# Key and value weights loaded ahead of the rope rows, a spread moved behind another row's products, two rows normalised in halves, and new rank offsets in a planned single-core decoder block

## The chip, the core and the metric

The kernel runs on one core of a Trainium2 chip. The time is the device time of one execution in microseconds; the median of several executions is what counts. PE is the matrix engine (TensorE), PEld its weight loads, DVE the vector engine, ACT the scalar engine, POOL the general-purpose vector engine (GpSimd), and SP the queue that issues nearly all transfers. Each of them works through its own list in the written order.

## The reference

One decoder block on x of 1024 rows by 1024 columns, all in float32:

```
h = RMSNorm(x)
qa, ka, va, q_lat, kv_lat, k_r, g_a, g_b = split(h @ w_in)      # 512|128|128|384|256|32|1024|1024
A = sliding-window attention(rope(qa), rope(ka), va, sinks)       # window 128, 8 heads on 2 key heads
q = RMSNorm(q_lat) @ w_uq        # 8 heads x (64 plain + 32 rope), rope on the 32
k, v = RMSNorm(kv_lat) @ w_ukv   # 8 heads x (64 key + 64 value); one 32-wide rope key for all heads
B = causal attention([q, rope q], [k, rope k_r], v)
x = x + (sigmoid(g_a) * (A @ w_o_swa) + sigmoid(g_b) * (B @ w_o_mla)) @ w_out
x = x + (silu(RMSNorm(x) @ w_gate) * (RMSNorm(x) @ w_up)) @ w_down
out = RMSNorm(x)
```

## The kernel before

Every large product is done in three passes (`mm3`, lines 311 to 313 of the profile). An operand is split into a high part, which ACT writes as a rounded copy (`CAST`), and a low part, the difference, which DVE (sometimes POOL) writes; PE then multiplies high by high, high by low and low by high into one PSUM bank. Larger matrix products also use a seven-product scheme, whose sums and differences of blocks are DVE and POOL work. The 1024 rows of x are eight blocks of 128, called rows 0 to 7 here.

The order of work is written down by a planner, the class `Plan`. A step has a name such as `("nm", 1)`, an engine (E for PE, A for ACT, D for DVE, P for POOL, S for SP, J for a bookkeeping step that emits nothing), a cost, the steps that it comes after, a rank, and the buffers that it takes and gives back. `run` keeps a clock for each engine, and always emits the step that could start first; among those that could start within a slack of each other it takes the one with the lowest rank. Costs, ranks and the constants `TAIL` and `HOP` (what an engine's end and a hand-over are reckoned at) therefore only set the order of instructions in each engine's list. There are three plans, one behind the other:

- `beg`, the first 305 us of the span: the normalisation of x, the latent query rows, the projections, the gates and the sliding-window attention. Here the ranks come from the time by which a step is needed, and the table `SHIFT` adds an offset for each kind of step.
- `pre`, the next 33 us or so: transposes of the latent rows (`lT`), the rope part of the queries (`r`, then `ra`, `rj`, `rq`), splits of the query weights (`a`) and of the key and value weights (`b`), the last gates, and the first query product. Its ranks are a position plus the offset in `PRANK`.
- `plan`, up to about 530 us: the latent attention with its scores (`scb`), softmax (`p`), transposes (`pTb`), output products (`ob`), and the products that make queries, keys and values, with the table `RANK`.

The rest of the span (output projections and the feed-forward part) is not touched.

In the start of `beg` a row b is treated thus. ACT sums its squares (`sq`); POOL makes a diagonal matrix of the reciprocal root (`dg`, line 866); PE multiplies ones by it and so spreads the factors over all partitions into a bank `rb` (`sp`, line 852); DVE multiplies the transposed row `xt` by it (`nm`, line 855); ACT and DVE split the result in two halves of four 128-blocks of the contraction each (`bh` and `bl`, tiles `hh` and `hl`); and PE multiplies the pieces with the query-latent weights in four steps of six matmuls (`qf`, the last one `ql`). Rows 0 and 4 are multiplied raw, ahead of their normalisation. The rows come in the order 0, 4, 1, 5, 2, 6, 3, 7.

In `pre`, `("ld", "ukv", k)` loads half of the key and value weights (`wr<-in_w_ukv_dram`, line 401), `b` splits it into the tiles `wv` and `wk`, `rd` stores the rotated query rows to a scratch array `rq_d`, `R` (line 1675) loads them into the query tiles `qT`, `rt` loads the rope tables, `gs` stores gates, `xd` copies the rope key to the other key tiles, and `lf` gives the latent rows' buffers back.

## Time and profile before

| | us |
|---|---|
| median of 3 runs (1315.77 to 1316.03) | 1315.99 |
| profiled execution | 1316.1 |
| its span | 1314.4 |
| PE busy | 1297.5 (99%), 6223 matmuls |
| PE weight loads busy | 1086.3 (83%) |
| DVE busy | 958.5 (73%) |
| ACT busy | 653.5 (50%) |
| POOL busy | 514.7 (39%) |
| mean granted PE clock | 0.995 |

The share of an engine is its busy time over the span; a share says nothing on which stage the engine waits in, so stretches of the span are looked at apart. A window row gives a stretch, its length, busy time and number of instructions of each engine, the PE clock that was granted in it (1.00 is full speed), the DMA share and GB/s. In a timeline row, what stands in brackets is the idle time of the engine just before the instruction, and the instruction that ended it. Matmuls are pipelined, so their durations overlap: the distance of two starts is what one takes.

### The profile page before, as it was taken

How to read it: one execution, taken by the hardware profiler on the slowest of the kernel's cores; microseconds unless marked ns; L12 is line 12 of the kernel's file. 1: busy time of each engine (PE TensorE's matmuls, PEld its weight loads, DVE VectorE, ACT ScalarE, POOL GpSimd, SP SyncE). 2: the span in 40 equal slices, each digit the busy share in tenths (PEclk: the TensorE clock that was granted, in tenths of full speed). 3: DMA queues.
4: the chain of work that ended last, by engine and by line, in shares of the span. 5: the costliest groups of instructions: out<-in, count | busy, mean ns of one | idle time of the engine just before them, and what ended most of it. 6: DMA issues, size and time to landing. Idle time of an engine off the chain costs nothing.

```text
span 1314.4 us, 18180 instructions
## 1 busy us (share of the span) xinstructions
PE 1297.5 (99%) x6223; PEld 1086.3 (83%) x6223; DVE 958.5 (73%) x1573; ACT 653.5 (50%) x1319; POOL 514.7 (39%) x468
## 2 busy tenths in 40 slices
PE   8999999999999999999999999999999999999997
PEld 6988888888788888888888888888888888888886
DVE  6998989976678885588889765766566555663964
ACT  6855766663577796544464232232323323644341
POOL 3211433432232266310234477775566621022521
PEclk9999999999899999999999999999999999999999
DMA  9312333343500023895231345743454335995504
GB/s 369 135 31 97 97 109 116 125 151 134 172 17 9 25 81 114 299 265 171 108 102 48 128 150 211 273 177 135 167 185 166 131 126 201 387 380 202 177 15 145
DMA packets 79835, 201.53 MB, mean 153 GB/s; under 512 B 10176, under 2 KB 16832, under 8 KB 79040
## 3 DMA queue, kind: packets, MB, share of 16 engines
q1 hardware_dynamic: 76864, 193.57, 41.5%
q0 software_dynamic: 1440, 4.72, 1.8%
q10 hardware_dynamic: 1440, 2.10, 0.4%
q8 instruction: 49, 0.80, 0.3%
q14 instruction: 42, 0.34, 0.1%
HBM read 138.88 MB, written 57.28 MB: 149 GB/s over the span
## 4 chain that ended last, share of the span: by engine, by line
PE 97%; DVE 1%; ACT 1%; issue 1%; DMA 0%; POOL 0%; ACTq 0%; DVEq 0%
PE fa L311 8%; PE fa L313 8%; PE fa L312 8%; PE fb L311 6%; PE fb L313 6%; PE fb L312 6%; PE fd L313 5%; PE fd L312 5%; PE fd L311 5%; PE pTb L1908 2%; PE xo L313 2%; PE st L311 2%; PE st L312 2%; PE st L313 2%; PE xo L311 2%; PE xo L312 2%
## 5 line engine op out<-in xcount | busy, mean ns | idle before, releaser
L305 DVE TENSOR_TENSOR wl<-wr,wl 128x512 fp32r<-128x512 f32 x110 | 116.9, 1092 | 53.7 <-ACT wl L304 53.7
L305 DVE TENSOR_TENSOR lrv<-lr,lrv 128x1024 fp32r<-128x1024 f32 x77 | 104.9, 1396 | 48.9 <-ACT lrv L304 46.6
L304 ACT CAST lrv<-lr 128x1024 fp32r<-128x1024 f32 x77 | 80.1, 1052 | 94.4 <-PE fd L313 60.7
L311 PE MATMUL fd<-lrv 128*128 128x512 f32 x308 | 119.8, 389 | 0.0
L312 PE MATMUL fd<-lrv 128*128 128x512 f32 x308 | 119.8, 389 | 0.0
L313 PE MATMUL fd<-lrv 128*128 128x512 f32 x308 | 119.8, 389 | 0.0
L1892 POOL TENSOR_SCALAR p<-p,denb 128x384 f32<-128x384 f32 (+3 forms) x64 | 47.7, 750 | 96.2 <-DVE denb L1888 77.1
L312 PEld LDWEIGHTS fd<-lrv 128*128 128x128 f32 x308 | 57.8, 188 | 12.1
L311 PEld LDWEIGHTS fd<-lrv 128*128 128x128 f32 x308 | 57.8, 188 | 12.0
L319 POOL TENSOR_TENSOR wr<-wr,sm 128x512 f32<-128x512 f32 x20 | 30.6, 1530 | 94.9 <-DVE wl L305 94.9
L313 PEld LDWEIGHTS fd<-lrv 128*128 128x128 f32 x308 | 57.8, 188 | 11.9
L304 ACT CAST wl<-wr 128x512 fp32r<-128x512 f32 x110 | 62.2, 618 | 0.7 <-DMA rb_d<-wd 0.7
L305 DVE TENSOR_TENSOR wl<-sm,wl 128x512 fp32r<-128x512 f32 x44 | 41.5, 976 | 27.9 <-ACT wl L304 27.9
L2371 ACT ACTIVATE act<-sm 128x512 f32<-128x512 f32 x11 | 7.0, 632 | 104.1 <-DVE sm L316 104.1
L316 DVE TENSOR_TENSOR ptl<-pTb,pth 128x512 fp32r<-128x512 f32 (+2 forms) x96 | 50.0, 550 | 10.2 <-ACT pth L1919 8.7
L1883 ACT ACTIVATE p<-scb,nmb 128x384 f32<-128x384 f32 (+3 forms) x64 | 48.0, 751 | 12.0 <-DVE nmb L1878 8.9
L1878 DVE CUSTOM_DVE_ANT_0 scb<-scb,mask 128x384 f32<-128x384 f32 (+3 forms) x64 | 48.2, 760 | 6.7 <-PE scb L1865 6.4
L1919 ACT CAST pth<-pTb 128x512 fp32r<-128x512 f32 (+2 forms) x96 | 43.0, 485 | 10.5 <-PE pTb L1908 10.1
L2371 ACT ACTIVATE act<-pu 128x512 f32<-128x512 f32 x22 | 13.9, 632 | 66.6 <-DVE pu L316 34.0
L311 PE MATMUL fb<-t3h,wl 128*128 128x512 f32 x120 | 47.0, 392 | 0.0
L311 PE MATMUL fb<-t2h,wl 128*128 128x512 f32 x120 | 47.0, 391 | 0.0
L313 PE MATMUL fb<-t2h,wl 128*128 128x512 f32 x120 | 46.8, 390 | 0.0
(435 smaller groups left out, 4234.2 us busy)
## 6 DMA issues: line engine op xcount, KB each, us to landing
lr<-la_d SPq DMA_DIRECT2D x77, 256.0 KB, 5.4
wr<-in_w_gate_dram SPq DMA_DIRECT2D x22, 512.0 KB, 4.6
wr<-in_w_up_dram SPq DMA_DIRECT2D x22, 512.0 KB, 5.1
la_d<-sd SPq DMA_DIRECT2D x22, 512.0 KB, 5.5
wd<-in_w_down_dram SPq DMA_DIRECT2D x22, 512.0 KB, 7.0
rb_d<-wd SPq DMA_DIRECT2D x22, 512.0 KB, 2.7
lr<-rb_d SPq DMA_DIRECT2D x44, 256.0 KB, 5.4
lr<-in_w_down_dram SPq DMA_DIRECT2D x33, 256.0 KB, 5.4
```

The lines of the kernel that those rows point to most:

```text
L304: nc.scalar.copy(hi, src)
L305: (eng or nc.vector).tensor_tensor(lo, src, hi.bitcast(F32), op=ALU.subtract)
L311: nc.tensor.matmul(ps, ah, bh, start=first and i == 0, stop=False, skip_group_check=go_on)
L312: nc.tensor.matmul(ps, ah, bl, start=False, stop=False, skip_group_check=go_on)
L313: nc.tensor.matmul(ps, al, bh, start=False, stop=last and i == n - 1, skip_group_check=go_on)
L316: eng.tensor_tensor(out, a, b, op=ALU.subtract)
L319: eng.tensor_tensor(out, a, b, op=ALU.add)
L1878: nc.vector.tensor_tensor_reduce(s_, s_, m_, 1.0, -NEG, op0=ALU.add, op1=ALU.min, accum_out=nm)
L1883: nc.scalar.activation(p_, s_, AF.Exp, scale=-1.0, bias=t_.pop(("nm", key)), accum_out=den)
L1892: nc.gpsimd.tensor_scalar(p[:, 0:w], p[:, 0:w], den, 0.0, op0=ALU.mult, op1=ALU.add)
L1908: nc.tensor.transpose(pp[:, k], t_["p", key][:, blk(4 * g + k)], ident)
L1919: nc.scalar.copy(hi, pp)
```

## The change

Tables: `SHIFT`, `PRANK` and `RANK` get other values for some kinds of steps, and `SHIFT` gets offsets for seven more kinds. Steps: rows 1 and 5 (`HALVED`) are normalised by two instructions of 512 elements in place of one of 1024, the first as a new step `nh`, and the first-half splits wait for `nh` alone; the spread of row 5 comes after `("qf", 1, 1)`, the second of row 1's four latent-query pieces. In `pre`, SP's reckoned end and four transfer costs change, and `lf` is no longer a step of SP. What is multiplied and added stays the same.

```
-    SHIFT = {'bh': -5100, 'km': 1000, 'qT': -2100, 'pv': -3400, 'k4': -6200, ...
+    HALVED = (1, 5)
+    SHIFT = {'bh': -5100, 'km': 13900, 'qT': 1900, 'pv': -40300, 'k4': -6200, ...
...
-    def normalize(b):
-        nc.vector.tensor_tensor(xt[b], xt[b], rb.pop(b).unsqueeze(1).to_broadcast([P, NK, P]), op=ALU.mult)
+    def normalize(b, k0=0, k1=NK):
+        t = xt[b][:, k0:k1]
+        nc.vector.tensor_tensor(t, t, rb[b].unsqueeze(1).to_broadcast([P, k1 - k0, P]), op=ALU.mult)
+        if k1 == NK:
+            rb.pop(b)
...
-        go("sp", b, eng="E", cost=250, emit=lambda b=b: spread_row(b), after=[("dg", b), ("L", "x", b)] + [("sp", 7)] * (b == 4), take=("p", ("rb", b), 0))
+        go("sp", b, eng="E", cost=250, emit=lambda b=b: spread_row(b), after=[("dg", b), ("L", "x", b)] + {4: [("sp", 7)], 5: [("qf", 1, 1)]}.get(b, []), take=("p", ("rb", b), 0))
...
-        go("nm", b, eng="D", cost=1300, emit=lambda b=b: normalize(b), after=[("sp", b), *raw_lo] + [("h0", 1)] * (b == 0), give=("rb", b))
+        if b in HALVED:
+            go("nh", b, eng="D", cost=690, emit=lambda b=b: normalize(b, 0, 4), after=[("sp", b)])
+        go("nm", b, eng="D", cost=690 if b in HALVED else 1300, emit=lambda b=b: normalize(b, 4 * (b in HALVED)),
+           after=[("nh" if b in HALVED else "sp", b), *raw_lo] + [("h0", 1)] * (b == 0), give=("rb", b))
...
-                quad_steps(b, kh, ("bh", "bl"), [("nm", b)] + [("ql", b)] * (b in RAWS))
+                quad_steps(b, kh, ("bh", "bl"), [("nm" if kh else "nh", b) if b in HALVED else ("nm", b)] + [("ql", b)] * (b in RAWS))
...
-    PRANK = {... 'k': -3.46, ... 'gs': -1.91, 'ra': 3.13, 'xd': 0.35, 'ld': 2.52, ... 'c': -4.22, ... 'rd': 4.2, ...
+    pre.TAIL = {**Plan.TAIL, "S": 2500, "J": 0}
+    pre.HOP = {**Plan.HOP, "J": 0}
+    PRANK = {... 'k': -14.76, ... 'gs': -23.71, 'ra': -75.67, 'xd': -0.85, 'ld': -32.68, ... 'c': -93.82, ... 'rd': -0.0, ...
...
-        pre_step("rd", s, x=x + 3, eng="S", cost=3000, emit=store, after=[("rql", s)], free=(("rq", s),))
+        pre_step("rd", s, x=x + 3, eng="S", cost=3600, emit=store, after=[("rql", s)], free=(("rq", s),))
...
-        pre_step("lf", s, x=0, eng="S", cost=1, emit=lambda: None, free=[("lat", 4 * s + b) for b in range(4)],
+        pre_step("lf", s, x=0, eng="J", cost=0, emit=lambda: None, free=[("lat", 4 * s + b) for b in range(4)],
...
-    RANK = {... 'E': 4.12, ... 'Q': 1.9, ... 'Ql': 1.26, 'K': -3.3, ...
+    RANK = {... 'E': -1.88, ... 'Q': -1.8, ... 'Ql': -2.14, 'K': -0.3, ...
```

The costs of `gs` (400 to 3500), `R` (3000 to 4800) and `xd` (3000 to 4600) change in the same way as that of `rd`.

PE's list in the start of `beg`, around the spread of row 5 (the second `rb`; `ql` with `hh_8` is row 4's product, with `hh_2` row 1's). Before:

```order
L312 MATMUL ql_34_201<-wv_37_226,hh_8_126 128x416
L313 MATMUL ql_34_201<-wv_37_226,hl_9_127 128x416
L852 MATMUL rb_44_273<-dg_1_115 128x128
L311 MATMUL ql_46_278<-wv_28_177,hh_2_120 128x416
L312 MATMUL ql_46_278<-wv_28_177,hh_2_120 128x416
L313 MATMUL ql_46_278<-wv_28_177,hl_3_121 128x416
```

And with the change:

```order
L313 MATMUL ql_34_201<-wv_37_226,hl_9_127 128x416
L311 MATMUL ql_44_274<-wv_28_177,hh_2_120 128x416
L312 MATMUL ql_44_274<-wv_28_177,hh_2_120 128x416
L313 MATMUL ql_44_274<-wv_28_177,hl_3_121 128x416
L311 MATMUL ql_44_274<-wv_28_177,hh_2_120 128x416
L312 MATMUL ql_44_274<-wv_28_177,hh_2_120 128x416
L313 MATMUL ql_44_274<-wv_28_177,hl_3_121 128x416
L311 MATMUL ql_44_274<-wv_31_189,hh_2_120 128x416
L312 MATMUL ql_44_274<-wv_31_189,hh_2_120 128x416
L313 MATMUL ql_44_274<-wv_31_189,hl_3_121 128x416
L311 MATMUL ql_44_274<-wv_31_189,hh_2_120 128x416
L312 MATMUL ql_44_274<-wv_31_189,hh_2_120 128x416
```

One more matmul of row 1 follows, and then the spread of row 5: it has moved behind the first twelve matmuls of row 1.

SP's list in `pre`, around the store of the rope rows (`rq_d<-rq`), their loads (`qT`) and the loads of key and value weights (`wr<-in_w_ukv_dram`). Before:

```order
L1597 DMA rq_d<-rq_3530 256x1x512 [waits Pool_49]
L1597 DMA rq_d<-rq_3530 256x1x512 [waits DMAHW0_49]
L1709 DMA gate_d<-go_3436 128x512 [waits DVE_49]
L401 DMA wr_3642<-in_w_ukv_dram 128x1024 [waits DMAHW2_49,PE_49]
L1709 DMA gate_d<-go_3561 128x512 [waits DMAHW3_49,DVE_49]
L401 DMA wr_3666<-in_w_ukv_dram 128x1024 [waits DMAHW5_49,DMAHW4_49,DMAHW1_49]
L1675 DMA qT_3603<-rq_d 16x2x512 [waits DMAHW7_49]
```

And with the change:

```order
L1718 DMA gate_d<-go_3469 128x512 [waits DMAHW6_49,Activation_49]
L401 DMA wr_3520<-in_w_ukv_dram 128x1024 [waits DMAHW7_49,PE_49]
L401 DMA wr_3571<-in_w_ukv_dram 128x1024 [waits DMAHW0_49,DMAHW1_49,DVE_49,PE_49]
L1606 DMA rq_d<-rq_3569 256x1x512 [waits Pool_49]
L1606 DMA rq_d<-rq_3569 256x1x512 [waits DMAHW2_49]
L1684 DMA qT_3635<-rq_d 16x2x512 [waits DMAHW3_49,DMAHW1_49,PE_49]
```

The two loads of key and value weights now stand ahead of the store of the rope rows, and next to each other; before, they stood behind it.

DVE's list in the sliding-window attention, at the query of block 10 (`qs`, two rows) and a rope step of a block's projected keys (`rp`, `w1`). Before:

```order
L319 TENSOR_TENSOR go_394_2508<-fb_354_2271,pu_353_2269 128x512
L1108 TENSOR_TENSOR qs_393_2505<-qT_390_2481,qs_393_2505 64x2x128
L1109 TENSOR_TENSOR qs_393_2505<-qT_390_2481,qs_393_2505 64x2x128
L316 TENSOR_TENSOR wl_395_2512<-sm_392_2489,wl_395_2512 128x512
L316 TENSOR_TENSOR wl_396_2517<-wr_364_2335,wl_396_2517 128x512
L319 TENSOR_TENSOR go_394_2508<-fa_375_2397,pu_353_2269 128x512
L316 TENSOR_TENSOR wr_355_2284<-wr_355_2284 128x512
L475 TENSOR_TENSOR rp_404_2562<-w1_116_861,tab_81_561 128x256 x2
L477 TENSOR_TENSOR w1_116_861<-rp_404_2562 128x4x32
L478 TENSOR_TENSOR w1_116_861<-rp_404_2562 128x4x32
```

And with the change:

```order
L319 TENSOR_TENSOR go_391_2503<-fb_352_2269,pu_358_2301 128x512
L475 TENSOR_TENSOR rp_394_2508<-w1_114_864,tab_84_580 128x256 x2
L477 TENSOR_TENSOR w1_114_864<-rp_394_2508 128x4x32
L478 TENSOR_TENSOR w1_114_864<-rp_394_2508 128x4x32
L316 TENSOR_TENSOR ptl_393_2506<-pT_390_2485,pth_392_2505 128x512
L316 TENSOR_TENSOR wl_395_2516<-wr_360_2311,wl_395_2516 128x512
L319 TENSOR_TENSOR go_391_2503<-fa_378_2412,pu_358_2301 128x512
L316 TENSOR_TENSOR wl_397_2524<-wr_354_2287,wl_397_2524 128x512
L1115 TENSOR_TENSOR qs_399_2541<-qT_396_2520,qs_399_2541 64x2x128
L1116 TENSOR_TENSOR qs_399_2541<-qT_396_2520,qs_399_2541 64x2x128
```

The rope steps have moved ahead: before, the query of block 10 stood ahead of the next-to-last of them (the one shown), and now it stands behind the last one (shown) and behind the transposed probabilities of block 8 (`ptl`).

## The prediction

> **What bounds the kernel now.** I read the windows first, since one share for a span of 1314.4 us says nothing on where a change can pay. The columns are the stretch, its length, then busy time of PE, PEld, DVE, ACT and POOL, the granted PE clock, the DMA share and GB/s.

> ```profile
> 16.72:20.13 3.41, 1.10 (x7) 0.88 (x6) 2.06 (x5) 2.19 (x4) 1.88 (x2) 1.00 1.02 407
> 20.13:23.55 3.42, 3.42 (x11) 3.28 (x11) 3.36 (x7) 2.52 (x5) 1.62 (x3) 0.50 1.03 379
> 23.55:60.00 36.45, 36.45 (x188) 34.17 (x188) 33.77 (x54) 31.06 (x65) 12.89 (x19) 1.00 0.62 227
> 60.00:130.00 70.00, 70.00 (x321) 58.24 (x320) 63.49 (x137) 38.66 (x92) 10.78 (x11) 1.00 0.19 59
> 130.00:205.00 75.00, 74.52 (x380) 62.19 (x379) 68.52 (x168) 52.86 (x169) 27.92 (x38) 1.00 0.29 96
> 205.00:250.00 45.00, 45.00 (x226) 37.54 (x225) 43.46 (x92) 30.55 (x91) 17.89 (x23) 1.00 0.39 128
> ...
> 305.00:337.57 32.57, 32.50 (x167) 26.81 (x165) 20.30 (x33) 13.44 (x24) 10.15 (x9) 1.00 0.51 165
> 337.57:340.98 3.41, 0.84 (x3) 0.30 (x2) 2.24 (x5) 3.25 (x6) 1.46 (x1) 1.00 0.27 103
> 340.98:344.40 3.42, 2.81 (x7) 2.15 (x8) 1.76 (x3) 0.68 (x3) 0.00 (x0) 0.50 1.06 229
> 344.40:347.81 3.41, 3.41 (x10) 2.64 (x9) 2.07 (x3) 1.08 (x2) 0.00 (x0) 0.50 0.55 190
> ...
> 369.00:480.00 111.00, 108.92 (x714) 96.74 (x713) 93.36 (x236) 86.38 (x198) 39.13 (x49) 1.00 0.12 38
> ```

> PE is busy without a break in most stretches, so nothing done to another engine pays unless PE stops waiting for it. PE has two holes, 16.72:20.13 (busy 1.10) and 337.57:340.98 (busy 0.84). After each the clock is 0.50, for 3.42 us and for 6.83 us. A third, thin loss is spread over 369:480 (2.08 us not busy). The waits of PE name what ended these holes (us in total, times, longest):

> ```profile
> PE k L311 <- ACT wv L1552: 2.3, 1, 2.3
> PE rb L852 <- POOL dg L866: 2.3, 1, 2.3
> ...
> PE k L313 <- DVE wv L316: 0.9, 1, 0.9
> PE pTb L1908 <- DVE qT L2007: 0.8, 2, 0.4
> PE pTb L1908 <- DVE kT L316: 0.7, 2, 0.3
> ```

> The first hole at the seam into the attention is the key product waiting for the split key/value weights (`wv`). The hole at the start is the spread of row 5 (`rb`, L852) waiting for row 5's diagonal (`dg`). These two parts I cost from the timelines (start, duration, engine, operation).

> **Part 1, the start.** Before, PE's queue holds the spread of row 5 ahead of row 1's latent-query matmuls, though these need only row 1.

> ```profile
> 16.40 0.35 PE L312 MATMUL ql<-wv,hh 128*128 128x416 f32 x1
> 16.59 0.35 PE L313 MATMUL ql<-wv,hl 128*128 128x416 f32 x1
> 19.25 0.49 PE L852 MATMUL rb<-dg 128*128 128x128 f32 x2 [2.31 <-POOL dg L866]
> 20.14 0.55 PE L311 MATMUL ql<-wv,hh 128*128 128x416 f32 x1
> 20.49 0.55 PE L312 MATMUL ql<-wv,hh 128*128 128x416 f32 x1
> ...
> 15.84 1.22 DVE L855 TENSOR_TENSOR xt<-xt,rb 128x1024 f32<-128x1024 f32 x1 [2.14 <-PE rb L852]
> 21.03 0.69 DVE L316 TENSOR_TENSOR xt<-xt,xt 128x512 f32<-128x512 f32 x1
> ...
> 21.03 0.62 ACT L746 CAST hh<-xt 128x512 fp32r<-128x512 f32 x1 [1.75 <-DVE xt L855]
> ...
> 17.88 1.32 POOL L866 TENSOR_SCALAR dg<-ident,rn 128x128 f32<-128x128 f32 x1
> ```

> What is lost: the starts 16.59 and 19.25 stand 2.66 us apart where the pitch is 0.19, so 2.47; then nine matmuls at a pitch of 0.35 instead of 0.19, so 1.44; with refilling about 0.1. Together 4.0 us.

> After, the spread of row 5 stands behind twelve matmuls of row 1 (12 x 0.19 = 2.3 us). Its diagonal, done at 19.2, is then there before PE is. What is late next is row 1 itself. Normalised in halves, its first half costs what a 128x512 operation costs, 0.69, and ends near 16.5; the copy of 0.62 gives `hh` near 17.2 and the subtraction of 0.69 gives `hl` near 17.9. DVE does the second half in between, so the added halves cost 2 x 0.69 - 1.22 = 0.16 each, twice, on a DVE that idles there anyway (2.14 before its first normalisation). PE would have gone on at 16.8: it waits about 0.3 for `hh` and, two matmuls later, 0.35 for `hl`. This is too little to lower the clock if the row below is a guide: there PE was busy 2.92 of a 3.41 us window and kept 1.00.

> ```profile
> 183.97:187.38 3.41, 2.92 (x15) 2.13 (x14) 2.60 (x7) 3.30 (x9) 2.15 (x3) 1.00 0.77 245
> ```

> PE now runs 3.3 us ahead of before, but the loads do not: the DMA share is 1.02 and 1.03 in both windows above, so rows arrive as they did. The window 23.55:60 had no PE wait; the spread of row 0, row 5's second pieces, the bank that the latent-scaling step frees, and row 7's spread and pieces each become a wait of 0.3 to 0.45, by laying the old landing and finishing times against the new PE times. I take 1.7 for these. Bounds: nothing is given back (gain 4.0) and everything is (gain 0, or 0.5 of loss if the first-half chain is slower than its rows). Taken: 4.0 - 0.65 - 1.7 = **-1.7 us**.

> **Part 2, 60 to 305.** The new `SHIFT` offsets move no matmul work in or out; they reorder DVE, ACT, POOL and SP. In 60:130 and 205:250 PE has no wait, so nothing can be gained there. In 130:205 PE is not busy for 75 - 74.52 = 0.48. Against this, the key-rope steps of the sliding-window part now stand earlier on DVE, so that the query (`qs`), transposed-probability (`ptl`) and gate steps of the middle blocks have 4 to 10 us more work ahead of them (the DVE order of the change, each step with its old duration), the most at block 8. One such rope step is the first two of these rows, 1.9 us of DVE; the other two show a `ptl` and the product that uses it:

> ```profile
> 171.22 0.75 DVE L475 TENSOR_TENSOR rp<-w,tab 128x256 f32<-128x256 f32 x2
> 172.22 1.13 DVE L478 TENSOR_TENSOR w<-rp 128x128 f32<-128x128 f32 x1
> ...
> 200.00 0.68 DVE L316 TENSOR_TENSOR ptl<-pT,pth 128x512 fp32r<-128x512 f32 x1
> ...
> 206.12 0.39 PE L1206 MATMUL o<-pth,vv 128*128 128x512 f32 x1
> ```

> It is the same work in another place. This `ptl` ends at 200.68, 5.4 us before its use at 206.12; other steps had some 3 us. DVE was not busy for 75 - 68.52 + 45 - 43.46 = 8.0 us over 130:250, which can soak up part. I cannot see that exactly: bounds are a gain of 0.7 (the old waits go) and a loss of 3 (10 us less half of these 8.0 and a margin of 3, lost once). Nearer the first, since work moved ahead is missing later, and PE stood still only for 0.48 with this DVE: **0**.

> **Part 3, rope rows and key/value weights.** SP issues all transfers in written order, and waits with each.

> ```profile
> 337.29 0.39 PE L313 MATMUL q<-cq,wuq 128*128 128x512 f32 x1
> 340.00 0.50 PE L311 MATMUL k<-ckv,wv 128*128 128x512 f32 x1 [2.31 <-ACT wv L1552]
> 342.18 0.63 PE L311 MATMUL k<-ckv,wv 128*128 128x512 f32 x1
> 347.73 0.43 PE L312 MATMUL k<-ckv,wv 128*128 128x512 f32 x1
> ...
> 338.82 2.17 ACT L1552 CAST wv<-wr 128x512 fp32r<-128x512 f32 x4
> ...
> 340.26 2.48 DVE L316 TENSOR_TENSOR wv<-wr,wv 128x512 fp32r<-128x512 f32 x4
> ...
> 326.55 1.29 SPq L1597 DMA_DIRECT2D rq_d<-rq  x2
> 328.86 1.14 SPq L401 DMA_DIRECT2D wr<-in_w_ukv_dram  x1
> 332.59 0.33 SPq L401 DMA_DIRECT2D wr<-in_w_ukv_dram  x1
> ...
> wr<-in_w_ukv_dram SPq DMA_DIRECT2D x2, 512.0 KB, 6.1
> ```

> The second weight half is issued at 332.59, 6.1 us to land, then 2.17 of casts and 2.48 of subtractions: the key product cannot start before 340. Between the starts 337.29 and 347.73 lie 17 matmul steps, 3.9 us at a pitch of 0.23 (0.19 x 512/416), and 10.44 were taken: 6.5 us lost, of which about 2.6 (13 x 0.2) is the half clock.

> After, both weight loads stand on SP ahead of the rope store (two transfers) and the rope rows (four). The first waits for a transpose that PE ends near 316, the second for a rope product that ends near 321 (the PE order of the change, with the old durations). By the 6.1 they land near 323 and 327, and the 4.65 of splits, as two halves beside other work of ACT and DVE (13.44 and 20.30 busy of 32.57), end near 331. PE wants them at 337, so this wait goes with 6 us to spare, and the half clock with it.

> Moved back, behind the second weight load: the rope store of part 0 and its four row loads. The store's rows are ready at 326.55; its issue then starts at 326.5 or at once behind the load, not later than before by more than the 0.33 of one issue, and the rows follow 4 to 5 us later, near 335, the first scores needing them at 341. The wait is covered by 6 us; without this cover the first score would stall instead of the key product (a rival below). The two bookkeeping steps moved off SP, and the changed costs of the stores, emit no instruction. Bounds: -6.5 (all goes) and -1.5 (a new wait takes the hole's place, with its cold clock, and only the second wait and part of the half clock go). Taken, by the nearer row: **-6.5**.

> **Part 4, the attention's ranks.** Query and key products and their splits change places. The listed waits on `kT` (0.7) should go, as the key products come earlier by the new order; those on `qT` (0.8) stay. Bounds -2.0 (all not-busy time in 369:480) and +1 (two new waits of the same size). Taken: **-0.7**.

> **Sum.** -1.7 + 0 - 6.5 - 0.7 = -8.9. The profiled execution took 1316.1 us (1.7 outside its span), 0.1 over the median of the runs shown, so 1316.0 - 8.9 = **1307.1 us**.

> [...] Row first: an idle time of 2.31 in one window was followed by 0.50. [...]

> **Rivals.**
> - The half clock has another cause than the holes and stays. For it: the holes were 2.3 us long, shorter than the clock's own stretches of 3.4. Against: each slow stretch follows directly on a hole, and nowhere else. Gain without 1.44 and 2.6: 1307.1 + 4.0 = 1311.1. Chance 0.04. [...]
> - The DVE backlog of part 2 reaches PE once: +3, 1310.1. For it: DVE is 91% and 97% busy in 130:205 and 205:250. Against: PE stood still only for 0.48 there. Chance 0.17.
> - The seam's wait moves to the rope rows, or the start's gain goes into later loads: 1307.1 + 5 = 1312 for the first. For it: six transfers now stand behind a waiting load. Against: 6 us of cover. Chance 0.10.
> - The change does nothing that shows: both a new wait at the seam and the backlog, 1314 to 1316. Chance 0.04.
> - Slower: the backlog does not drain. At block 8 it is 10 us; if the DVE's idle time gives back under half of it, PE waits in holes of 2.3 us, each followed by a half-clock stretch of 3.42 (1.7 lost), 4.0 a piece. From the third on (12 against 8.9) the kernel is slower; three give 1307.1 + 12 = 1319. For it: 0.97 busy DVE in 205:250. Against: 3 to 5 us of margin at the users. Chance 0.05.

> **How the numbers follow.** The forecast has 0.60. Its own range, from the bounds of parts 1, 2 and 4, is 1304 to 1309.5. To hold 8 in 10 I add the backlog and part of the seam case: 1303 to 1312.5. The bound for no change is 0.2% (2.6 us), about what a measurement of this kernel can tell: faster means under 1313.4. Forecast, the first two rivals and most of the third give 0.87; same 0.07; slower 0.06.

> **What would show it.** Right, if the profile after has no half clock near 20 and 341, the spread of row 5 behind twelve matmuls, small waits of 0.3 to 0.5 between 17 and 50, the key/value weight issue before 322, and no wait of PE on `wv`. Wrong, if PE waits over 1 us on `qT` or `kT` rope rows near 341, on `qs`, `ptl` or gate steps in 150:250, or if the clock is 0.50 anywhere after warm-up.

## The result, and the profile after

| | before | after |
|---|---|---|
| median of 6 runs each, us | 1315.74 (1314.30 to 1316.03) | 1305.57 (1304.62 to 1305.64) |
| profiled execution, us | 1316.1 | 1305.36 |
| its span, us | 1314.4 | 1303.6 |

The ratio is 0.9924 (95% interval 0.9911 to 0.9936): 10.2 us less, where 8.9 was predicted. In a later set of runs it was 0.9929 (0.9917 to 0.9942), 1305.19 against 1314.67. One run of the kernel before, among those that the experiments below share, took 1658.76 us at a granted clock of 0.732, and no ratio includes it. The same stretches of the span, after:

```profile
16.72:20.13 3.41, 3.03 (x16) 2.66 (x16) 1.70 (x5) 2.13 (x5) 2.35 (x4) 1.00 1.02 408
20.13:23.55 3.42, 2.99 (x18) 2.63 (x17) 3.38 (x6) 3.42 (x8) 1.29 (x2) 1.00 1.03 367
...
130.00:205.00 75.00, 75.00 (x383) 63.10 (x382) 70.54 (x171) 50.33 (x158) 27.50 (x36) 1.00 0.32 101
205.00:250.00 45.00, 44.57 (x222) 37.07 (x221) 42.02 (x90) 32.99 (x98) 20.39 (x26) 1.00 0.36 120
...
305.00:337.57 32.57, 32.57 (x162) 26.81 (x161) 25.41 (x38) 15.85 (x29) 11.72 (x8) 1.00 0.52 161
337.57:340.98 3.41, 3.41 (x18) 2.89 (x16) 3.31 (x7) 2.37 (x5) 0.00 (x0) 1.00 0.99 370
340.98:344.40 3.42, 3.42 (x16) 2.59 (x15) 2.25 (x5) 1.90 (x5) 0.59 (x1) 1.00 0.25 73
```

Both holes are gone, and no stretch between the warm-up and PE's last matmul is at 0.50 (only the last 4.8 us of the span are, in which PE has nothing left to do; before, the last 4.0). The seam is without a break. What the start gained came in part back as smaller waits; here are all the waits of PE in the changed kernel, the warm-up's left out:

```profile
PE pTb L1917 <- DVE qT L2016: 0.8, 2, 0.4
PE ob L1954 <- DVE ptl L316: 0.6, 1, 0.6
PE ql L889 <- DMA wr<-in_w_ql_dram: 0.5, 1, 0.5
PE rb L853 <- POOL dg L870: 0.4, 1, 0.4
PE fa L311 <- ACT pu L682: 0.4, 1, 0.4
PE ql L311 <- ACT hh L747: 0.3, 1, 0.3
```

To see what each stage lost, I add up by how much each matmul ended later than the usual distance for its shape (0.227 us for 512 columns) after the one before it:

| stage, by the work in it | lost before, us | lost after, us |
|---|---|---|
| 0 to 60 (start) | 8.5 | 6.4 |
| 130 to 300 (sliding-window part) | 1.9 | 1.9 |
| 300 to the end of the second half clock; after, to 337.5 (seam) | 7.1 | 0.4 |
| from there to 540; after, to 529 (latent attention) | 7.2 | 4.9 |

That is -2.1, 0, -6.7 and -2.3, and together 11.1; the spans differ by 10.8. What is taken as the usual distance moves single sums by some tenths of a microsecond, so here is the same between fixed points: from the last product ahead of the start's hole to the first gate product PE took 111.6 us before and 109.6 after, from there to the first score of the latent attention 220.1 and 213.6, and from there to the end of the span 966.1 and 964.1. That is -2.0, -6.5 and -2.0.

### The profile page after: what moved, and what is told of

Read it like the earlier page. It is cut to its first block, busy times and chain, and to the rows that moved or that the text cites. A ratio compares the mean times of both kernels' runs of the same rounds, so it can differ in the third digit from the quotient of the medians.

```text
span 1303.6 us, 18164 instructions
## 1 busy us (share of the span) xinstructions
PE 1291.9 (99%) x6223; PEld 1082.0 (83%) x6223; DVE 958.1 (73%) x1575; ACT 656.2 (50%) x1319; POOL 513.9 (39%) x468
## 4 chain that ended last, share of the span: by engine, by line
PE 94%; DVE 3%; ACT 1%; DMA 1%; issue 1%; POOL 0%; SPq 0%; ACTq 0%; DVEq 0%
PE fa L311 8%; PE fa L313 8%; PE fa L312 8%; PE fb L313 6%; PE fb L311 6%; PE fb L312 6%; PE fd L313 5%; PE fd L311 5%; PE fd L312 5%; PE pTb L1917 2%; PE st L313 2%; PE st L312 2%; PE xo L312 2%; PE xo L313 2%; PE st L311 2%; PE xo L311 2%
## 5 line engine op out<-in xcount | busy, mean ns | idle before, releaser
L312 PE MATMUL fd<-lrv 128*128 128x512 f32 x308 | 119.9, 389 | 0.0
L311 PE MATMUL fd<-lrv 128*128 128x512 f32 x308 | 119.8, 389 | 0.0
L313 PE MATMUL fd<-lrv 128*128 128x512 f32 x308 | 119.8, 389 | 0.0
L312 PEld LDWEIGHTS fd<-lrv 128*128 128x128 f32 x308 | 57.8, 188 | 12.4 <-DVE lrv L305 0.4
L313 PEld LDWEIGHTS fd<-lrv 128*128 128x128 f32 x308 | 57.8, 188 | 12.0
L311 PEld LDWEIGHTS fd<-lrv 128*128 128x128 f32 x308 | 57.8, 188 | 11.9
L316 DVE TENSOR_TENSOR ptl<-pTb,pth 128x512 fp32r<-128x512 f32 (+2 forms) x96 | 49.5, 549 | 9.0 <-ACT pth L1928 8.6
L1892 ACT ACTIVATE p<-scb,nmb 128x384 f32<-128x384 f32 (+3 forms) x64 | 48.0, 750 | 10.8 <-DVE nmb L1887 8.0
L311 PE MATMUL fb<-t2h,wl 128*128 128x512 f32 x120 | 47.2, 393 | 0.0
L311 PE MATMUL fb<-t3h,wl 128*128 128x512 f32 x120 | 47.1, 392 | 0.0
L313 PE MATMUL fb<-t2h,wl 128*128 128x512 f32 x120 | 46.8, 390 | 0.0
## 6 DMA issues: line engine op xcount, KB each, us to landing
wr<-in_w_gate_dram SPq DMA_DIRECT2D x22, 512.0 KB, 4.4
wr<-in_w_up_dram SPq DMA_DIRECT2D x22, 512.0 KB, 5.0
la_d<-sd SPq DMA_DIRECT2D x22, 512.0 KB, 5.5
wd<-in_w_down_dram SPq DMA_DIRECT2D x22, 512.0 KB, 7.1
rb_d<-wd SPq DMA_DIRECT2D x22, 512.0 KB, 2.6
```

Of the source, the lines that this page charges most:

```text
L311: nc.tensor.matmul(ps, ah, bh, start=first and i == 0, stop=False, skip_group_check=go_on)
L312: nc.tensor.matmul(ps, ah, bl, start=False, stop=False, skip_group_check=go_on)
L313: nc.tensor.matmul(ps, al, bh, start=False, stop=last and i == n - 1, skip_group_check=go_on)
L316: eng.tensor_tensor(out, a, b, op=ALU.subtract)
L1892: nc.scalar.activation(p_, s_, AF.Exp, scale=-1.0, bias=t_.pop(("nm", key)), accum_out=den)
```

## Experiments: the parts apart

Each kernel is the one before with one part of the change. The first four shared 21 runs of the kernel before (median 1315.08).

**The middle plan alone** (`PRANK`, the four costs, SP's reckoned end, the bookkeeping step).

```
-    PRANK = {... 'ld': 2.52, ... 'rd': 4.2, ...
+    PRANK = {... 'ld': -32.68, ... 'rd': -0.0, ...
```

> The kernel before with only the middle plan's edits (PRANK, the four transfer costs, SP's reckoned end, the bookkeeping step off SP). Theory A (the seam's loss is the late issue of the second key/value weight load): 6.5 us less than before, about 1309.2, no PE wait on wv and no half clock at 341. Theory B (the wait moves to the rope rows, since in the whole change other offsets give the cover): about 3 to 4 us less, with a PE wait of over 1 us on qT or kT near 341.

Measured: 1308.52, ratio 0.9952 (0.9938 to 0.9966), 6.6 us less. PE's waits on `wv` are gone and none on the rope rows took their place, so theory A holds. The edit moves other steps of this plan too; what ties the gain to the loads is that the wait on `wv` is what went. In the changed kernel's timelines the mechanism reads as follows (in this kernel's own, the weight loads are issued by 319.2 and the key product starts at 335.15):

```profile
314.86 4.55 SPq L401 DMA_DIRECT2D wr<-in_w_ukv_dram  x2
324.11 1.29 SPq L1606 DMA_DIRECT2D rq_d<-rq  x2
327.35 2.59 SPq L1684 DMA_DIRECT2D qT<-rq_d  x4
...
323.74 1.67 ACT L1561 CAST wv<-wr 128x512 fp32r<-128x512 f32 x3
...
327.02 2.88 DVE L316 TENSOR_TENSOR wv<-wr,wv 128x512 fp32r<-128x512 f32 x2
...
335.45 0.39 PE L311 MATMUL k<-ckv,wv 128*128 128x512 f32 x1
...
339.53 0.34 PE L1872 MATMUL scb<-kT,qT 96*128 96x384 f32 x1
```

Both weight loads are issued by 319.4, the splits end at 329.9, and the key product at 335.45 has 5.5 us to spare. The rope rows' loads are issued by 329.94, 9.6 us before the first scores.

**The attention's ranks alone.**

```
-    RANK = {... 'E': 4.12, ... 'Q': 1.9, ... 'K': -3.3, ...
+    RANK = {... 'E': -1.88, ... 'Q': -1.8, ... 'K': -0.3, ...
```

> The kernel before with only the attention's RANK table of the change. The change showed about 2.5 us less in the attention where 0.7 was predicted. Theory A (the table alone does it): 2.5 us less than before, about 1313.2, seam unchanged with 6.5 us lost. Theory B (the table takes away only the listed waits on kT, 0.7, and the rest comes from the middle plan's leaving queues in another state): 0.7 less, about 1315.0.

Measured: 1313.03, ratio 0.9984 (0.9975 to 0.9993), 2.1 us less. The interval leaves room for 0.9 to 3.3, so the time alone would hardly speak against 0.7; the profile does. The latent attention lost 5.0 us by the sum above, nearly as in the whole change (4.9), against 7.2 before. Runs at about the same granted clock say the same: of the 21 runs of the kernel before, the eight at 0.994 or 0.995 took 1315.7 on average, and the eight of this one at 0.995 took 1313.3. Theory A holds. Where the rest beyond the waits on `kT` may have been is seen in the waits of PE's weight loads (PEld), which the prediction left out. Before, 348 to 480:

```profile
PEld pTb L1908 <- PE pTb L1908: 2.3, 4, 0.6
PEld scb L1863 <- ACT p L1883: 1.5, 6, 0.4
```

and after, in the same stage, 338 to 470 (`pTb` is a transposition, `scb` a score):

```profile
PEld scb L1872 <- ACT p L1892: 1.3, 4, 0.4
PEld pTb L1917 <- PE pTb L1917: 1.2, 2, 0.6
PEld ob L1954 <- DVE ptl L316: 0.9, 1, 0.9
```

The four waits that make up 2.3 are PE's listed ones on `qT` and `kT`, at the same times, but 0.53 to 0.60 each where PE's list has 0.33 to 0.39. So these listed waits are dearer than the list says, and the two on `kT` were worth 1.1, not 0.7. From start to start it is the same: at a wait on `qT` of 0.39 the two starts are 0.66 apart, where two such transpositions usually stand 0.11 apart. In all, this view lists 5.7 before and 3.7 after, with a new wait of 0.9 for an output product (`ob`) already counted in. At the wait on `qT`, before, the weight load starts at 448.40, after a wait of 0.59, the matmul follows at 448.44, and of the 0.66 between the two starts 0.27 counts as busy, up to the modelled end of the matmul before; so PE lists 0.39 where 0.66 - 0.11 = 0.55 is lost. The author's reading of the other waits is the same, also where PE lists none. The 2.0 us fit the measured gain; no run takes these waits away by themselves, so this part is argued.

**The start's two step edits alone**, all tables as before.

```
+    HALVED = (1, 5)
...
-  ... + [("sp", 7)] * (b == 4), take=("p", ("rb", b), 0))
+  ... + {4: [("sp", 7)], 5: [("qf", 1, 1)]}.get(b, []), take=("p", ("rb", b), 0))
```

> The kernel before with only the start's two step edits: the spread of row 5 behind row 1's second piece, rows 1 and 5 normalised in halves. All tables (SHIFT, PRANK, RANK) as before. Theory A (the start's gain is the removed hole and its half clock, less small new waits, and needs no offsets): 2.0 us less than before, so about 1313.7 against 1315.7, no half clock near 20 us. Theory B (the loads set the pace of the first 60 us, and what PE gains is given back unless the offsets reorder the rest): within 0.5 us of before.

Measured: 1328.22, ratio 1.0100 (1.0086 to 1.0114), 13 us more. Neither theory had this. The start itself is as hoped (7.2 us lost in the first 60, against 8.5), but 14.9 us were lost between 130 and 200. In PE's timeline of this kernel the attention steps stand one behind the other, with no gate product (`fa`, `fb`) between:

```profile
177.83 0.39 PE L313 MATMUL fa<-hh,wl 128*128 128x512 f32 x1
178.06 1.11 PE L1134 MATMUL sc<-khd,qs 128*128 128x256 f32 x8
179.01 0.38 PE L1104 MATMUL qT<-ident,qn 128*128 128x128 f32 x2
179.26 0.44 PE L502 MATMUL kT<-ident,kd 128*128 128x128 f32 x2
180.72 0.44 PE L1104 MATMUL qT<-ident,qn 128*128 128x128 f32 x2 [1.03 <-DMA qn<-q_d]
182.63 0.50 PE L1213 MATMUL o<-pth,vv 128*128 128x512 f32 x1 [1.47 <-DVE khd L316]
...
183.67 1.11 PE L1134 MATMUL sc<-khd,qs 128*128 128x256 f32 x8
184.61 0.38 PE L1104 MATMUL qT<-ident,qn 128*128 128x128 f32 x2
189.75 1.09 PE L1183 MATMUL pT<-ident,pe 128*128 128x128 f32 x4 [4.76 <-DVE oa L1230]
190.63 0.77 PE L311 MATMUL fa<-hh,wl 128*128 128x512 f32 x1
```

Before, PE's list here has a gate product after every one or two of these steps: score 5, gate 14, query transpose 6, gate 15, key transpose 6, output 4, gate 16. In this kernel it has score 5, query transpose 6, key transpose 5, query transpose 7, output 3, score 6, query transpose 8 and probability transpose 4 in a row. They hang on each other through transfers and the work of other engines: in the rows above PE waited 1.03 for a query (`qn`), 1.47 for a key (`khd`) and 4.76 for `oa`, and its list had no gate product to go on with in these places. The longest hole emptied a whole stretch, and two stretches at 0.50 followed:

```profile
185.16:188.57 3.41, 0.00 (x0) 0.00 (x0) 3.23 (x8) 2.55 (x7) 0.41 (x1) 1.00 0.06 22
188.57:191.98 3.41, 2.23 (x7) 1.88 (x8) 3.16 (x10) 2.18 (x10) 1.49 (x3) 0.50 0.00 0
191.98:195.40 3.42, 3.42 (x9) 2.65 (x8) 2.16 (x5) 0.00 (x0) 0.76 (x1) 0.50 0.39 158
```

**The offsets alone.**

```
-    SHIFT = {... 'qT': -2100, 'pv': -3400, ... 'sp': -3000, ...
+    SHIFT = {... 'qT': 1900, 'pv': -40300, ... 'sp': -55600, ...
```

> The kernel before with only the new SHIFT offsets; no halves, no condition on the spread of row 5, PRANK and RANK as before. Theory A (the offsets are worth nothing): within 0.7 us of before, the hole of 2.3 us at the spread of row 5 and its half clock still there. Theory B (the moved key-rope work ahead of query and probability steps costs, and the start's gain hides it in the whole change): 1.5 to 3 us more than before, with PE waits of over 1 us between 150 and 250.

Measured: 1316.89, ratio 1.0012 (1.0003 to 1.0021), 1.8 us more; its hole at the spread of row 5 is still there. The waits that theory B wanted between 150 and 250 are not: the longest there is 0.6 us. What is new are waits in the first 60 us, `ql` on `hl` (0.8), and between 25 and 60 us the sum over matmuls is 1.9 us, where it was 0 before. So neither theory holds as it stood: the offsets alone do cost, but in the start.

**Step edits and offsets together**, that is, the whole of the first plan. This, the next two and the kernel of the next section shared 27 runs of the kernel before (1314.9).

> The kernel before with the whole of the first plan's change: halves, the spread of row 5 behind row 1's second piece, and the new SHIFT. PRANK and RANK as before. The step edits alone made 13 us more, the offsets alone 1.8 more. Theory A (the offsets fit the edited steps; together they give what the whole change shows in its first 300 us): 1.0 to 1.8 us less than the 1315.1 before, about 1313.7, no PE wait over 1 us ahead of the seam, the seam's 6.5 us still lost. Theory B (in the whole change the later plans hide a loss here): as slow as before or slower.

Measured: 1313.46, ratio 0.9988 (0.9979 to 0.9997), 1.4 us less: theory A. The three plans, each alone, gave 6.6, 2.1 and 1.4 us less, 10.1 together, against 10.2 for the whole: within the noise they add. Within the first plan nothing adds: +13 and +1.8 make -1.4.

**Each step edit by itself**, old tables: first the spread behind row 1's second piece.

> The kernel before with only the spread of row 5 behind row 1's second piece; no halves, tables as before. The two step edits together made 13 us more, by PE waits between 164 and 195. Theory A (any new timing of the start upsets the list of the sliding-window part, which the old offsets fit): also over 5 us more than before, with PE waits of over 1 us between 150 and 200. Theory B (the halved steps do it, since the new step nh has no offset in the old table): at the start PE waits 0.7 us longer for row 1 than in the version with halves, no long wait later, about 1 us less than before.

Measured: 1314.70, ratio 0.9999 (0.9990 to 1.0008): no difference, and no wait over 0.5 us between 150 and 200, as theory B has it; the gain of about 1 us that B also wanted does not show. The hole of 2.31 became a wait of 0.8 for row 1's `hh`, and 0.4 and 0.9 at later spreads.

Then the halves.

> The kernel before with only rows 1 and 5 normalised in halves; the spread of row 5 is placed by the planner, and stands behind six matmuls of row 1; tables as before. Theory A (any new timing upsets the sliding-window part): over 5 us more than before, PE waits between 150 and 200. Theory B (the two edits need each other for the loss): within 2 us of before; the hole at the spread of row 5 is 1.2 us shorter, so its window stays at full clock.

Measured: 1331.21, ratio 1.0121 (1.0108 to 1.0135), 16 us more, 13.5 of it lost between 130 and 200 and 7.1 between 25 and 60. So neither theory holds for both: the spread alone does no harm, and the halves alone cost more than both edits together. Whether the extra step, its cost (690 twice in place of 1300) or the earlier first-half splits turn the list, no run here separates.

**The step edits with one offset of the new table**, with 15 other runs of the kernel before (1314.67).

```
-    SHIFT = {... 'qT': -2100, ...
+    SHIFT = {... 'qT': 1900, ...
```

> The two step edits of the start with the old SHIFT table, but for one offset: qT (query transposes) 1900 as in the change, where it was -2100. With the old offset these edits made 13 us more, and PE's list had the transposes of blocks 6, 7 and 8 close together with no gate product between them and the attention steps of blocks 3 to 6. With qT later, gate products stand between them again. Theory A (that crowding is the whole loss): 13 us less than start_only, 1.0 to 1.8 less than before, no PE wait over 1 us between 150 and 200. Theory B (the loss comes from more than the transposes): PE waits of over 1 us remain there, and the time is over 1317.

Measured: 1316.03, ratio 1.0012 (1.0003 to 1.0021). No wait over 1 us is left between 150 and 200: the crowding was some 12 of the 13 us, and the 4000 added to the query transposes undoes it. In PE's timeline between 171 and 198 us a gate product of twelve matmuls stands again behind every one to three of the steps. It is not the whole: this is 1.4 above the kernel before, not below, so neither theory holds in full. The new waits that remain are 1.0 and 0.6 for `hl` in the first 60 us and 0.6 for a key (`kd`) behind 150.

**The same with the other two plans**, and the whole change beside it.

> The same (step edits of the start, old SHIFT but for qT), with the change's PRANK, transfer costs, bookkeeping and RANK. Alone, the middle plan's edits gave 6.6 less and RANK 2.1 less. Theory A (the parts add): 1305.0 to 1306.0, the same as the whole change, so that of the offsets only qT is needed. Theory B (the other offsets are worth something behind the start): 1 us or more above the whole change.

> The changed kernel as it is, on the same chip as the two others. Both theories: 0.992 to 0.993 of before, about 1305.5.

Measured: 1307.61, 0.9948 (0.9935 to 0.9962), against 1305.19, 0.9929 (0.9917 to 0.9942), for the whole. Theory B: the other offsets are worth about 2.4 us. Of the 1.1 us by which the profiled spans differ, the sum over matmuls puts 0.5 in 0 to 60 and 0.9 in 130 to 300, and gives 0.3 back in the attention. Of all versions the whole change is the fastest.

## Experiment: the clock by itself

This kernel fills the holes of the kernel before with matmuls whose results are overwritten.

```
+        for _ in range(12 if b == 5 else 0):
+            nc.tensor.matmul(rb[b], ones, dg[:, 1], start=True, stop=True)
         nc.tensor.matmul(rb[b], ones, dg[:, b if b < 7 else 1], start=True, stop=True)
...
+            for _ in range(10 if (j, s) == (0, 0) else 0):
+                nc.tensor.matmul(ps, wuq[0][0][:, 0, 0], cq[0][0][:, half(0)], start=True, stop=True)
```

> The kernel before with extra matmuls whose results are overwritten: twelve 128x128 ones into the bank of row 5's spread just ahead of it, and ten 128x512 ones into the bank of the first key product just ahead of it. They fill the two holes of 2.3 us and wait for nothing new. Theory A (the clock falls because PE is busy for less than about half of one of the clock's 3.41 us stretches): the holes cost what they did, but no half clock follows; 2.6 to 2.9 us less at the seam, and at the start 1.4 in those runs whose stretches lie so that the hole counted (about two in three): about 1311.4. Theory B (the half clock has another cause): about 1315, half clock at both places.

Measured: 1312.50, ratio 0.9981 (0.9972 to 0.9989), 2.4 us less, and no half clock between the warm-up and PE's last matmul. Its rows at the two places:

```profile
16.61:20.02 3.41, 3.41 (x30) 3.41 (x29) 2.32 (x4) 2.19 (x4) 1.89 (x2) 1.00 1.03 410
20.02:23.44 3.42, 3.42 (x21) 3.38 (x21) 3.02 (x5) 1.80 (x4) 1.38 (x2) 1.00 1.04 360
...
340.88:344.29 3.41, 3.17 (x14) 2.26 (x13) 1.56 (x4) 1.75 (x3) 0.00 (x0) 1.00 0.88 192
```

PE's other waits are as before to within 0.3 us, but for one of 0.7 on query weights at 8 us, which comes and goes between kernels of the same start (none before, 0.4 in the middle plan alone). So this is the price of the clock alone, and the rival that the half clock has another cause is out. In these two profiles the price is near what was predicted: from the last product ahead of the start's hole to the first gate product PE took 111.6 us before and 110.1 here, and from there to the first score 220.1 and 217.7, so 1.45 and 2.4, where 1.44 and 2.6 were reckoned. The median moved less than that: 2.4, where 3.6 was expected. The profiles show a reason: the stretches of 3.41 us lie differently in each (the figures are in the last section). In the profile of the middle plan alone, whose start has the same list, the same hole of 2.31 us lay across two stretches, with PE busy for 1.80 and 2.71 us, and no half clock followed:

```profile
14.47:17.88 3.41, 1.80 (x11) 1.44 (x9) 2.09 (x4) 2.49 (x5) 1.24 (x2) 1.00 1.03 412
17.88:21.29 3.41, 2.71 (x15) 2.69 (x16) 2.67 (x5) 1.66 (x4) 1.46 (x2) 1.00 1.01 399
21.29:24.70 3.41, 3.41 (x21) 3.38 (x20) 3.31 (x6) 3.30 (x9) 2.07 (x4) 1.00 1.05 341
```

At the seam the half clock lasted one stretch in some profiles (3.42 us in the offsets alone, 3.41 in the spread alone) and two in others (6.83 before, 6.82 in the ranks alone). So the profile of before showed the dear case at both places, one slow stretch at the start and two at the seam, with a time of 1316.1; three later sets of runs of that kernel had medians of 1314.67 to 1315.08, and spread over 2.5 to 3.8 us. The granted clock of each of these runs shows the same: of the 62 that took under 1320 us, 19 had 0.994 or 0.995, as the profile had, and took 1314.8 to 1316.5; 37 had 0.996 or 0.997 and took 1313.9 to 1315.2; five had 0.998 and took 1312.5 to 1313.5. One, with 0.945 and 1315.58, fits no group.

## Why the prediction came out as it did

- **Seam, -6.5:** right in mechanism and size (6.7 by the sum, 6.6 alone). The issue came before 319.4, where 321 was reckoned, and the loads landed 3.4 us after it, where 6.1 was taken from the profile of before, so the cover was wider than reckoned; that of the rope rows held too.
- **Start, -1.7:** 2.1 by the sum, 1.4 alone. The first waits came where they were put: 0.30 for `hh`, 0.25 for `hl` (the starts 17.31 and 17.75 against a pitch of 0.19), 0.43 for the spread of row 0. From the last product ahead of the hole (in the changed kernel, of the wait for `hh`) to the seventeenth behind it PE took 7.56 us before and 4.35 after, 3.2 less, where 3.35 was reckoned; up to the first gate product 1.2 of that was given back, where 1.7 was reckoned. The step that was too sure is "Together 4.0 us": its 1.44 of half clock was lost in the profile of before, where one stretch held the hole (busy 1.10), and not in that of the middle plan alone, where two shared it (1.80 and 2.71). In the middle plan alone, which has the old start but no half clock in its profile, PE reached the first gate product in 110.0 us, so against that the new start (109.6) gains 0.4, and against the profile of before 2.0.
- **Offsets, 0:** the middle stages lost 1.9 before and after, as forecast, and no wait between 150 and 250 is over 0.43, so DVE's later steps did not reach PE. But the 0 as the price of the offsets was luck. I costed them against the old list, as if they could cost or be worth nothing; the step edits without them are 13 us slower, so here they are worth some 14.5. I priced DVE's order and left out PE's: the backlog rival looked for late DVE steps, and what went wrong without the offsets was the missing filler between PE's steps. Holes followed by half clock, the slower rival's mechanism, are just what that kernel shows (PE busy 0.00 in one stretch, and 6.8 us of half clock behind it).
- **Ranks, -0.7:** right in sign, too small by a factor of three (2.1 alone, 2.3 by the sum). The step that failed was to count "listed waits on `kT` (0.7)": a listed wait was not priced from start to start, by which these two were 1.1, and the other waits of the weight loads (PEld), 0.9 less in all, were left out.
- **The clock:** the rival that kept the half clock, with 1311.1, is shown wrong: with the holes filled the half clock did not come. A hole shorter than a stretch was enough: 2.31 us, with PE busy for 1.10 of the stretch's 3.41, were followed by 0.50.
- The sum was 1.3 us short of the measured gain, which is about the ranks' 1.4 to 1.6.

## What to carry to other kernels

In a kernel that one engine bounds, price each hole as the wait, plus the refill from start to start, plus the slow clock behind it (here two holes of 2.3 us, and 1.45 and 2.4 of slow clock); and read the waits of the weight loads with those of the matmuls. Where a planner writes the lists, an edit of one early step can turn the order far behind it (here the halves in the first 60 us, and the order from 160 us on): compare the bounding engine's own list there, and ask whether filler still stands between steps that depend on each other. A profiled run can show the dear case of a clock that falls or not with the phase of its stretches (here 1316.1, where later sets had medians of 1314.67 to 1315.08); a kernel with the same start tells, or more runs with their granted clocks.

## What the runs showed of the clock

What followed went with PE's busy time within a stretch, not with the length of a hole alone: the same hole of 2.31 us at the start was followed by 0.50 before (busy 1.10) and not in the middle plan alone (1.80 and 2.71). In the rows of these profiles, stretches at full clock were followed by 0.50 with 0.00 and 1.53 us busy (the step edits alone), 0.73 (the offsets alone, and the spread alone), 0.84 and 1.10 (before), 1.11 (the ranks alone, 336.92:340.34), 1.56 (the halves alone), 1.70 (step edits and offsets together) and 1.79 (the step edits with one offset). They were followed by full clock with 1.61 (the step edits with one offset), 1.64 (the halves alone), 1.71 (the offsets alone), 1.80 (the middle plan alone, and the step edits alone), 1.85 (step edits and offsets together), 2.36 (the step edits alone) and 2.51 (the holes filled); in the profiles of before and after every one with 2.77 or more was. So from 1.61 to 1.79 both occur. Two rows from the halves alone show one of each kind, each with the stretch behind it:

```profile
171.75:175.17 3.42, 1.64 (x8) 1.17 (x8) 2.82 (x14) 3.17 (x13) 0.58 (x2) 1.00 0.59 159
175.17:178.58 3.41, 2.79 (x12) 2.32 (x13) 0.57 (x1) 0.31 (x1) 2.83 (x4) 1.00 0.11 35
192.23:195.65 3.42, 1.56 (x10) 1.22 (x9) 3.20 (x10) 2.54 (x12) 1.90 (x3) 1.00 0.54 176
195.65:199.06 3.41, 3.41 (x11) 2.71 (x10) 3.25 (x10) 2.60 (x8) 2.25 (x3) 0.50 0.00 0
```

In these rows coming back took more than staying: at full clock 1.80 was followed by full clock twice, but at half clock stretches with 2.23 us busy (the step edits alone), 2.79 (the ranks alone) and 2.81 (before, 340.98:344.40) were followed by another slow one. Those with 2.98 (the offsets alone, shown here), 3.05 (the spread alone), 3.22 (the halves alone) and 3.29 (the step edits alone) were followed by full clock:

```profile
341.91:345.33 3.42, 2.98 (x7) 2.32 (x8) 1.59 (x3) 0.85 (x2) 0.00 (x0) 0.50 1.03 218
345.33:348.74 3.41, 3.41 (x17) 2.87 (x17) 2.50 (x4) 1.94 (x4) 0.00 (x0) 1.00 0.54 181
```

Busy times are modelled, so these bounds are rough; why a stretch of 1.64 was followed by full clock (above) and one of 1.70 by half clock (step edits and offsets together, 337.52:340.93) stays open.
